# Latent attention on Trainium2: values as the stationary operand, outputs turned back to tokens by a copy and two transposes

## The chip, the cores and the metric

The kernel runs as one program on one core of a Trainium2 chip. The metric is the device time of one execution in microseconds (us); for a kernel the median of its runs is given. The core has five engines with instruction streams of their own, which meet only at semaphores: TensorE (PE, whose weight loads the profile lists apart as PEld), VectorE (DVE), ScalarE (ACT), GpSimd (POOL) and SyncE (SP, which issues most DMAs). Each engine runs its own stream in order.

## The reference

The reference is two networks, one behind the other, on 512 tokens of width 1024. The first is one block of retention and dilated attention with an MLP; the change doesn't touch it. The second has two layers (depth 2) that take the 512 tokens, called latents here, and 256 context tokens. In each layer four mixers of width 256 stand beside one another, and two of them are attention with four heads of 64 channels:

```python
def neighbourhood_attention(q, k, v, k_ctx, v_ctx, rpb, rows):      # "neighbour" unit
    ...
    p = jax.nn.softmax(jnp.concatenate([s_loc, s_ctx], axis=-1), axis=-1).astype(v.dtype)
    ...
    o = jnp.einsum('bhrqik,brikhd->brqhd', p_loc, v_band) + jnp.einsum('bhrql,blhd->brqhd', p_ctx, v_ctx)

def diff_attend(q1, q2, k1, k2, v, lam):                            # "differential" unit
    ...
    p = jax.nn.softmax(s1, axis=-1) - lam * jax.nn.softmax(s2, axis=-1)
    return jnp.einsum('bhqk,bkhd->bqhd', p.astype(v.dtype), v)

def diff_post(o, g, lam_init):
    y = rms_norm_2(o, g) * (1 - lam_init)
    return y.reshape(o.shape[0], o.shape[1], GROUP_W)
```

For 128 latent queries a neighbour unit has 256 local and 256 context keys, a differential unit 512 latent and 256 context keys. The output of the differential unit is then normalised per head (rms over its 64 channels). All of this is float32.

## The kernel before, in words

**Big products.** Nearly all of the time goes to the projections and MLPs. `mm3` (L214 to L218) computes each float32 product as three products of type fp32r, with both operands split into a high and a low part; these are the lines L216, L217 and L218 of the profile. Weights arrive by DMA in `wr`, ACT makes `wh` (L156) and DVE makes `wl` (L145).

**Attention on the latents.** `attention` (L1660) runs once in each layer and so twice in the program. `units` (L1625) walks over four heads, four blocks `qb` of 128 queries, and the two units neighbour and differential: 32 units in a layer, 64 in both. Each unit first makes its scores in PSUM (tiles `s`, lines L1448 to L1459 and L1520, fp32r products), takes the row maximum on DVE (L1452, L1461, L1521) and the exponential on ACT (L142, tiles `f`, `ne`, `wl` in SBUF), with the row sum beside it; a reciprocal on DVE (L1466, L1523) gives one over the sum. The differential unit joins its two maps on DVE (L152, `ne`).

Only two units later (`AHEAD = 2`) does the unit's second half run, `values`. `attend_values` (L1416) transposes the probabilities on PE, block by block of 128 keys (L1424, into PSUM tile `tr`, of which there are two buffers), copies them to SBUF (`wh`, L1426 on DVE or L1428 on ACT), and multiplies (L1430): the transposed probabilities of 128 keys by 128 queries are the stationary operand, and a slice of the values moves, 128 columns wide, which are two heads; half of the result, 64 columns, is then used. The product is float32, has four blocks of keys in a neighbour unit (`hc` or `big`, and `cvn`) and six in a differential unit (`vd`, `cvd`), and stands in the profile as two records for each instruction. Its result `po` has queries on partitions. DVE scales it by the reciprocal into `tok` in the neighbour unit (L1470, listed as L149), ACT in the differential unit (L1531, listed as L142), and ACT squares it (`nj`) for the norm, whose sum it reads out.

**Behind it.** `diff_norm` (L1540) scales the differential outputs, once for heads 0 to 2 and once for head 3. Then `gather` (L1688) transposes `tok` to channels on partitions (L1698) and the output projection begins, with the projected k-tiles that don't depend on attention first.

**Order.** The order in which `units` writes the work is not the order on the engines: the instructions of each engine are put in order when the program is built, by the framework's estimate of when each one could start. It is fixed from then on. The context's own attention (`context`, tiles `npt`, `cst`) uses the same functions earlier in the program, interleaved with projections.

Of the kernel before, what the change touches and what calls it, by code (L numbers as in the profile page):

```python
# [82 lines left out]
class Net:  # L83
# [1332 lines left out]
    def attend_values(self, e, vs, head, po, eng=None):  # L1416

        nk = e.shape[1] // P
        pt = self.t([P, nk, P], self.soft["pt"])
        for b0 in range(0, nk, 4):  # L1420
            n = min(4, nk - b0)
            tp = self.ps((P, n, P), "tr")
            for i in range(n):
                self.nc.tensor.transpose(tp[:, i], e[:, (b0 + i) * P:(b0 + i + 1) * P], self.ident)  # L1424
            if eng and b0 == 0:
                self.nc.vector.tensor_copy(pt[:, b0:b0 + n], tp)  # L1426
            else:
                self.nc.scalar.copy(pt[:, b0:b0 + n], tp)  # L1428
        for kb in range(nk):
            self.nc.tensor.matmul(po, lhsT=pt[:, kb], rhs=vs[kb][:, head // 2 * P:(head // 2 + 1) * P],  # L1430
                                  start=kb == 0, stop=kb == nk - 1)
        return po[:, head % 2 * 64:(head % 2 + 1) * 64]

    def neighbour(self, yn, head, qb, qn, kx, kc, st, vx, vc, bt, po):

        nc = self.nc
        pair, odd = divmod(head, 2)
        rs = slice(odd * 64, (odd + 1) * 64)
        (qh, ql), (kch, kcl) = qn[pair], kc[pair]
# [12 lines left out]
        nc.vector.tensor_reduce(out=sm[:, 0:1], in_=ps[:, nl:], axis=AX.X, op=ALU.min)  # L1452
        vs, low = vc, sm[:, 0:1]
        if nl:
            w0 = WINDOW[qb]
            kh, kl = [k.rearrange("p (r c) -> p r c", c=64)[:, :, w0:w0 + 32] for k in (kh2, kx[pair][1])]
            out = ps[:, :nl].rearrange("p (r c) -> p r c", c=32)
            mm(out, lhsT=qs2[:, qs], rhs=kh, start=True, stop=False)
            mm(out, lhsT=qh[odd][:, qs], rhs=kl, start=False, stop=True)  # L1459
            low = sm[:, 1:2]  # L1460
            nc.vector.tensor_tensor_reduce(  # L1461
                out=ps[:, :nl], in0=ps[:, :nl], in1=bt[:, (qb + 1) // 2].rearrange("p r c -> p (r c)"), scale=1.0,
                scalar=sm[:, 0:1], op0=ALU.add, op1=ALU.min, accum_out=low)
            vs = [vx[:, qb, 0], vx[:, qb, 1]] + vc
        self.act(e, ps, AF.Exp, bias=low, scale=-1.0, accum_out=sm[:, 5:6])
        nc.vector.reciprocal(out=sm[:, 6:7], in_=sm[:, 5:6])  # L1466

        def values():
            o = self.attend_values(e, vs, head, po, qb % 2)
            self.ts(yn[:, qb, head * 64:(head + 1) * 64], o, sm[:, 6:7], ALU.mult)  # L1470
        return values

# [35 lines left out]
    def differential(self, s, yd, ssq, head, qb, qst, kst, vs, c, po):  # L1508
        nc = self.nc
        nk = kst.shape[2]  # L1510
        cuts = [(k0, min(k0 + 512, nk)) for k0 in range(0, nk, 512)]
        qs = slice(qb * P, (qb + 1) * P)
        sm = self.t([P, 16], "dsm")
        em = []
        for mp in range(2):
            b = mp * 8
            e = self.t([P, nk], self.soft["e"][mp])
            ps = self.ps((P, nk), self.soft["s2"])
            for k0, k1 in cuts:
                nc.tensor.matmul(ps[:, k0:k1], lhsT=qst[:, mp, qs], rhs=kst[:, mp, k0:k1], start=True, stop=True)  # L1520
            nc.vector.tensor_reduce(out=sm[:, b + 2:b + 3], in_=ps, axis=AX.X, op=ALU.max, negate=True)  # L1521
            self.act(e, ps, AF.Exp, bias=sm[:, b + 2:b + 3], accum_out=sm[:, b + 3:b + 4])
            nc.vector.reciprocal(out=sm[:, b + 6:b + 7], in_=sm[:, b + 3:b + 4])  # L1523
            em.append(e)

        self.stt(sm[:, 15:16], sm[:, 14:15], c["nlam"], sm[:, 3:4], ALU.mult, ALU.mult)
        self.stt(em[0], em[1], sm[:, 15:16], em[0], ALU.mult, ALU.add)

        def values():
            o = yd[:, qb, head * 64:(head + 1) * 64]  # L1530
            self.act(o, self.attend_values(em[0], vs, head, po), scale=sm[:, 6:7])  # L1531
            junk = self.t([P, 64], "nj")
            self.act(junk, o, AF.Square, accum_out=ssq[:, head, qb:qb + 1])
            if head == 3 and qb == 0 and not s.ctx:
                self.diff_norm(s, yd, ssq, 0, 3)
            if head == 3 and qb == s.nt - 1:
                self.diff_norm(s, yd, ssq, 0 if s.ctx else 3, 4)
        return values

    def diff_norm(self, s, yd, ssq, h0, h1):  # L1540

        n = h1 - h0
        v = self.t([P, n, s.nt], "rs_vd")
        self.ts(v, ssq[:, h0:h1], -0.5 / 64, ALU.mult, -0.5 * EPS, ALU.add)
        r = self.rsqrt(v.rearrange("p h t -> p (h t)"), n * s.nt).rearrange("p (h t) -> p h t", h=n)
        for h in range(h0, h1):
            o = yd[:, :, h * 64:(h + 1) * 64]
            self.tt(o, o, r[:, h - h0].unsqueeze(2).to_broadcast([P, s.nt, 64]), ALU.mult)
# [76 lines left out]
    def units(self, s, c, po, st, more, vx, vc, vd, bts):  # L1625

        todo = []
        for head in range(4):
            if head == 0:
                ssq = self.t([P, 4, s.nt], "ssq")  # L1630
                t = self.t([P, 2, s.nt, 256], "tokc" if s.ctx else "tok")
                s.yn, s.yd = t[:, 0], t[:, 1]
            for qb in range(s.nt):
                i = 2 * (qb % 2)
                for unit in range(2):
                    if unit:
                        todo.append(self.differential(s, s.yd, ssq, head, qb, st[head][0], st[head][1], vd, c, po[:, i + 1]))
                    else:
                        todo.append(self.neighbour(s.yn, head, qb, s.qn, None if s.ctx else s.kv[0], self.ckv[0], st[head],
                                                   vx, vc, bts[head], po[:, i]))  # L1640
                    if len(todo) > AHEAD:
                        todo.pop(0)()
                    if qb == 0 and unit and head < 3:
                        more(head + 1)
                    yield
        for values in todo:
            yield values

    def context(self, s, c):

# [8 lines left out]

    def attention(self, s, l, c, ne):  # L1660
        self.soft = {"e": ("ne", "wl"), "s2": "s2", "s1": "s1", "pt": "wh"}
        self.open("soft", ne=ne, nsm=5, dsm=5, ssq=2, nj=2)
        self.psum(SOFT_PS)
        po = self.ps((P, 4, P), "po")
        ckv = self.ckv
        vc = [ckv[1][:, i] for i in range(2)]
        vd = [s.kv[3][:, i] for i in range(s.nt)] + [ckv[3][:, i] for i in range(2)]
        st, bts = s.st, [self.nbias(l, 0)]

        def more(head):  # L1670
            bts.append(self.nbias(l, head))
            st.append(self.stacks(s, head))
        todo = [v for v in self.units(s, c, po, st, more, s.kv[1], vc, vd, bts) if v]
        self.gather_start(s)
        for values in todo:
            values()
        self.close("soft")
        self.close("heads")
        self.psum(GEMM_PS)
# [249 lines left out]
```

## Time and profile before

| | before |
|---|---|
| median of 3 runs | 2801.17 us (2799.91 to 2804.06) |
| the profiled execution: its time, its span | 2802.46 us, 2800.7 us |
| granted TensorE clock, mean | 0.996 of full speed |
| busy share of the span: PE, PEld, DVE, ACT, POOL | 98%, 84%, 61%, 38%, 2% |
| DMA | 354.74 MB, mean 127 GB/s |

A row of a group view names line, engine, operation and tiles (out<-in), then the shape, the count, the busy time in us, the mean of one in ns, and the idle time of the engine just before, with what ended it. A row of a timeline gives the start in us from the beginning of the span, the time from there to the last end in us, the engine, the line, what it writes and reads, and how many instructions of one kind are merged in it; idle time before it stands in brackets with what ended it. PE's instructions overlap in such a row: the distance from one start to the next is what one costs, and the length of a single record is longer.

### The profile page before, as it was taken

The page shows a single profiled execution, that of the slowest core. Times are in us where ns is not written, and L with a number is a line of the kernel's source. Part 1 is how long each engine was busy: PE and PEld are TensorE (multiplying, and loading weights), DVE is VectorE, ACT ScalarE, POOL GpSimd, SP SyncE. Part 2 cuts the span into 40 slices and gives each one's busy share as a digit, 9 for nine tenths or more (in the row PEclk, how much of TensorE's full clock was granted, in tenths as well). Part 3 has the DMA queues.
Part 4 walks back from the last instruction along what each step waited for, and adds up shares of the span by engine and source line. Part 5 has one row for each costly group of instructions (what it writes and reads, how often), then busy time and mean ns, then how long its engine had stood idle before and what let it go on. Part 6 is the DMA issues. An engine that isn't in the chain of part 4 may idle for free.

```text
span 2800.7 us, 38389 instructions
## 1 busy us (share of the span) xinstructions
PE 2738.2 (98%) x15332; PEld 2354.6 (84%) x15332; DVE 1716.0 (61%) x3205; ACT 1057.5 (38%) x1969; POOL 62.3 (2%) x109
## 2 busy tenths in 40 slices
PE   8999999999999999999998999999999999999998
PEld 4888888988888888789887888888889988888887
DVE  6667777353567888788768564444446858644434
ACT  4433433333334223245647332222224538433323
POOL 3000000000020000000000000000000000000000
PEclk9999999999999999999999999999999999999999
DMA  7355343343354555755443421112122443323231
GB/s 273 127 198 165 136 152 128 120 127 97 116 180 163 181 185 196 236 168 169 136 116 89 128 62 61 61 61 73 63 68 92 133 134 93 126 95 102 91 105 61
DMA packets 275203, 354.74 MB, mean 127 GB/s; under 512 B 19320, under 2 KB 221170, under 8 KB 274768
## 3 DMA queue, kind: packets, MB, share of 16 engines
q1 hardware_dynamic: 259744, 323.58, 36.5%
q0 software_dynamic: 4384, 13.99, 1.6%
q10 hardware_dynamic: 10896, 14.72, 1.6%
q8 instruction: 121, 1.98, 0.3%
q14 instruction: 58, 0.48, 0.1%
HBM read 318.62 MB, written 23.65 MB: 122 GB/s over the span
## 4 chain that ended last, share of the span: by engine, by line
PE 83%; DVE 6%; DMA 4%; ACT 3%; issue 2%; POOL 1%; ACTq 0%; SPq 0%; DVEq 0%; POOLq 0%
PE mm L216 25%; PE mm L217 25%; PE mm L218 25%; DMA wr<-in_ada_w 2%; PE po L1430 2%; DVE ada L152 2%; DVE wl L145 1%; PE at L216 1%; ACT wh L156 1%; PE tr L1424 1%; DMA wr<-in_w_ff 1%; PE tr L398 1%; PE at L217 1%; PE at L218 1%; DVE dsm L1521 1%
## 5 line engine op out<-in xcount | busy, mean ns | idle before, releaser
L156 ACT CAST wh<-wr 128x1024 fp32r<-128x1024 f32 (+1 forms) x442 | 425.7, 970 | 822.3 <-PE mm L217 662.0
L145 DVE TENSOR_TENSOR wl<-wr,wh 128x1024 fp32r<-128x1024 f32 (+1 forms) x442 | 493.7, 1122 | 343.6 <-ACT wh L156 335.5
L216 PE MATMUL mm<-h,wh 128*128 128x512 f32 (+1 forms) x1712 | 652.1, 383 | 3.3 <-ACT h L142 2.4
L217 PE MATMUL mm<-h,wh 128*128 128x512 f32 (+1 forms) x1712 | 652.1, 382 | 0.4 <-DVE h L152 0.4
L218 PE MATMUL mm<-h,wl 128*128 128x512 f32 (+1 forms) x1712 | 650.3, 381 | 0.5 <-DVE wl L145 0.5
L216 PEld LDWEIGHTS mm<-h,wh 128*128 128x128 f32 x1712 | 321.6, 188 | 64.4 <-ACT h L142 3.5
L217 PEld LDWEIGHTS mm<-h,wh 128*128 128x128 f32 x1712 | 322.2, 188 | 62.6 <-DVE ada L152 3.4
L218 PEld LDWEIGHTS mm<-h,wl 128*128 128x128 f32 x1712 | 322.3, 188 | 60.3 <-DVE wl L145 0.9
L217 PE MATMUL mm<-mid,wh 128*128 128x512 f32 (+1 forms) x864 | 330.7, 383 | 0.9 <-DVE mid L145 0.9
L216 PE MATMUL mm<-mid,wh 128*128 128x512 f32 (+1 forms) x864 | 330.4, 383 | 0.0
L218 PE MATMUL mm<-mid,wl 128*128 128x512 f32 (+1 forms) x864 | 329.5, 381 | 0.0
L152 DVE SCALAR_TENSOR_TENSOR ada<-wr,cs,ada 128x1024 f32<-128x1024 f32 x168 | 212.4, 1279 | 37.0 <-DMA wr<-in_ada_w 25.3
L216 PE MATMUL mm<-wh,h 128*128 128x256 f32 x704 | 200.0, 284 | 0.0
L217 PE MATMUL mm<-wl,h 128*128 128x256 f32 x704 | 199.7, 284 | 0.0
L218 PE MATMUL mm<-wh,h 128*128 128x256 f32 x704 | 199.6, 284 | 0.0
L142 ACT ACTIVATE f<-mm 128x256 f32<-128x256 f32 (+2 forms) x192 | 99.5, 520 | 256.9 <-PE mm L218 256.7
L217 PEld LDWEIGHTS mm<-mid,wh 128*128 128x128 f32 x864 | 162.5, 188 | 32.9 <-DVE mid L145 2.2
L218 PEld LDWEIGHTS mm<-mid,wl 128*128 128x128 f32 x864 | 162.5, 188 | 31.1
L216 PEld LDWEIGHTS mm<-mid,wh 128*128 128x128 f32 x864 | 162.5, 188 | 30.6
L145 DVE TENSOR_TENSOR f<-f 128x512 f32<-128x512 f32 (+2 forms) x172 | 99.4, 585 | 143.5 <-ACT f L142 142.3
L152 DVE SCALAR_TENSOR_TENSOR x<-mm,modx,x 128x512 f32<-128x512 f32 (+1 forms) x116 | 84.8, 731 | 166.8 <-PE mm L218 165.4
L217 PEld LDWEIGHTS mm<-wl,h 128*128 128x128 f32 x704 | 134.8, 191 | 0.7 <-issue 0.2
(470 smaller groups left out, 4209.6 us busy)
## 6 DMA issues: line engine op xcount, KB each, us to landing
wr<-in_w_ff SPq DMA_DIRECT2D x96, 1024.0 KB
wr<-in_w_in SPq DMA_DIRECT2D x69, 1024.0 KB
wr<-in_ada_w SPq DMA_DIRECT2D x48, 1024.0 KB
wr<-in_w_ada SPq DMA_DIRECT2D x16, 1024.0 KB
wr<-in_w_in SPq DMA_DIRECT2D x24, 512.0 KB
awr<-in_w_ada SPq DMA_DIRECT2D x16, 512.0 KB
wr<-in_w_ret_out SPq DMA_DIRECT2D x8, 1024.0 KB
wr<-in_w_out SPq DMA_DIRECT2D x8, 1024.0 KB
```

The lines of the kernel that those rows point to most:

```text
L142: return self.nc.scalar.activation(out=out, in_=in_, func=func, **kw)
L145: return self.nc.vector.tensor_tensor(out=out, in0=a, in1=b, op=op)
L152: return self.nc.vector.scalar_tensor_tensor(out=out, in0=a, scalar=s, in1=b, op0=op0, op1=op1)
L156: self.nc.scalar.copy(hi, src)
L216: mm(out, lhsT=ah, rhs=bh, start=start, stop=False)
L217: mm(out, lhsT=ah, rhs=bl, start=False, stop=False)
L218: mm(out, lhsT=al, rhs=bh, start=False, stop=stop)
L398: when(self.nc.tensor.transpose(ps[:, j], acc[:, m * P:(m + 1) * P], self.ident))
L1424: self.nc.tensor.transpose(tp[:, i], e[:, (b0 + i) * P:(b0 + i + 1) * P], self.ident)
L1430: self.nc.tensor.matmul(po, lhsT=pt[:, kb], rhs=vs[kb][:, head // 2 * P:(head // 2 + 1) * P], start=kb == 0, stop=kb == nk - 1)
L1521: nc.vector.tensor_reduce(out=sm[:, b + 2:b + 3], in_=ps, axis=AX.X, op=ALU.max, negate=True)
```

## The change

For the latents (not the context), `attend_values` swaps the operands: 64 columns of the values, those of the one head, become the stationary operand, and the transposed probabilities move. The result has 64 channels on partitions and 128 queries in columns. The neighbour unit writes partitions 0 to 63 of `po`, the differential unit 64 to 127, and `po` holds four query blocks. The two scalings per block are gone. After every second block a new function, `token_major`, copies `po` of both units and two query blocks to SBUF on ACT (128x256), transposes it with two PE transposes into a `tr` buffer, and one DVE product with the reciprocals of both units (kept in a new tile `rden`) writes `tok`; ACT squares the differential half as before. The first part of `token_major`, the copy, follows the values at once; the transposes and what is behind them follow one unit later. `diff_norm` for heads 0 to 2 is called at the end of head 2.

```diff
@@ attend_values
+        turn = po.shape[0] == 64
+        cols = slice(head * 64, head * 64 + 64) if turn else slice(head // 2 * P, (head // 2 + 1) * P)
         for kb in range(nk):
-            self.nc.tensor.matmul(po, lhsT=pt[:, kb], rhs=vs[kb][:, head // 2 * P:(head // 2 + 1) * P],
-                                  start=kb == 0, stop=kb == nk - 1)
-        return po[:, head % 2 * 64:(head % 2 + 1) * 64]
+            a, b = pt[:, kb], vs[kb][:, cols]
+            if turn:
+                a, b = b, a
+            self.nc.tensor.matmul(po, lhsT=a, rhs=b, start=kb == 0, stop=kb == nk - 1)
+        return po if turn else po[:, head % 2 * 64:(head % 2 + 1) * 64]
@@ neighbour
-        nc.vector.reciprocal(out=sm[:, 6:7], in_=sm[:, 5:6])
+        nc.vector.reciprocal(out=self.rden[head % 2][:, qb, 0:1] if nl else sm[:, 6:7], in_=sm[:, 5:6])
         def values():
             o = self.attend_values(e, vs, head, po, qb % 2)
+            if nl:
+                return
             self.ts(yn[:, qb, head * 64:(head + 1) * 64], o, sm[:, 6:7], ALU.mult)
@@ differential
         def values():
+            if not s.ctx:
+                self.attend_values(em[0], vs, head, po)
+                return
...
+    def token_major(self, s, ssq, head, half, po):
+        nc = self.nc
+        ev = self.t([P, 2, P], "f")
+        nc.scalar.copy(ev, po[:, half])
+        yield
+        tp = self.ps((P, 2, P), "tr")
+        for i in range(2):
+            nc.tensor.transpose(tp[:, i], ev[:, i], self.ident)
+        qs = slice(half * 2, half * 2 + 2)
+        out = s.tok[:, :, qs, head * 64:(head + 1) * 64]
+        self.tt(out.rearrange("p u q r -> p q u r"), tp.rearrange("p q (u r) -> p q u r", u=2),
+                self.rden[head % 2][:, qs].unsqueeze(3).to_broadcast([P, 2, 2, 64]), ALU.mult)
+        junk = self.t([P, 2, 64], "nj")
+        o = out[:, 1]
+        for i in range(2):
+            self.act(junk[:, i], o[:, i], AF.Square, accum_out=ssq[:, head, half * 2 + i:half * 2 + i + 1])
+        if head == 2 and half:
+            self.diff_norm(s, s.yd, ssq, 0, 3)
+        if head == 3 and half:
+            self.diff_norm(s, s.yd, ssq, 3, 4)
+        yield
@@ units
+                    if turn:
+                        dst = po[unit * 64:(unit + 1) * 64, qb // 2, qb % 2]
...
+                    if back:
+                        next(back.pop(0))
@@ attention
-        self.open("soft", ne=ne, nsm=5, dsm=5, ssq=2, nj=2)
+        self.open("soft", ne=ne, nsm=5, dsm=5, ssq=2, nj=1, rden0=1, rden1=1)
...
-        po = self.ps((P, 4, P), "po")
+        po = self.ps((P, 2, 2, P), "po")
```

What this does to the order of PE is seen in the middle of the first layer's attention. Before, in one block of queries (PE; `po` is the product with the values, `tr` are transposes, `s` scores):

```order
L1430 MATMUL po<-hc,wh 128x128 x2
L1430 MATMUL po<-cvn,wh 128x128 x2
L1424 MATMUL tr<-ident,ne 128x128 x2
L1520 MATMUL s_13748<-h 128x256
L1448 MATMUL s_13718<-h 128x256
L1449 MATMUL s_13718<-ckn,qn 128x256
L1424 MATMUL tr<-ident,f 128x128 x3
L1430 MATMUL po<-vd,wh 128x128 x4
L1430 MATMUL po<-cvd,wh 128x128 x2
L1458 MATMUL s_13718<-h 128x256
```

Now, in the same block (L1435 is the product with the values, written 64x128; L1452 to L1463 and L1526 are the score lines, L1558 is the new transpose):

```order
L1435 MATMUL po<-wh,hc 64x128 x2
L1435 MATMUL po<-wh,cvn 64x128 x2
L1424 MATMUL tr<-ident,ne 128x128 x2
L1435 MATMUL po<-wh,vd 64x128 x4
L1526 MATMUL s_13752<-h 128x512
L1452 MATMUL s_13716<-h 128x256
L1453 MATMUL s_13716<-ckn,qn 128x256
L1435 MATMUL po<-wh,cvd 64x128 x2
L1526 MATMUL s_13752<-h 128x256
L1558 MATMUL tr<-ident,f 128x128 x2
```

The products with the values are now 64 columns wide and stand in three runs in this block, each with work of the full 128 columns before and behind it; before there were two runs, as wide as all else around them.

The second place is the end of the first layer's attention on DVE (`wl` is the weight split for the output projection, `rs_vd` begins the last `diff_norm`). Before:

```order
L149 TENSOR_SCALAR tok<-po,nsm 128x64 [waits PE_49,Activation_49]
L145 TENSOR_TENSOR hc<-yc,hc 128x256 x2
L145 TENSOR_TENSOR wl<-wr,wh 128x1024 [waits DMAHW6_49,Activation_49]
L145 TENSOR_TENSOR wl<-wr,wh 128x1024 [waits Activation_49]
L145 TENSOR_TENSOR wl<-wr,wh 128x1024 [waits DMAHW7_49,Activation_49]
L149 TENSOR_SCALAR rs_vd<-ssq 128x4 [waits Activation_49]
```

Now:

```order
L145 TENSOR_TENSOR wl<-wr,wh 128x1024 [waits DMAHW6_49,Activation_49]
L145 TENSOR_TENSOR wl<-wr,wh 128x1024 [waits Activation_49]
L145 TENSOR_TENSOR tok<-tr,rden_13285 128x2x2x64 [waits PE_49]
L145 TENSOR_TENSOR wl<-wr,wh 128x1024 [waits DMAHW7_49,Activation_49]
L149 TENSOR_SCALAR rs_vd<-ssq 128x4 [waits Activation_49]
```

The last writing of `tok` has moved from ACT (and, for the neighbour unit, from ahead of the weight splits) to DVE behind two weight splits, and the squares that feed `rs_vd` wait for it.

## Rows read from the trace of the kernel before

**Rows 1.** The page's busy times and shares of the span.

```profile
PE 2738.2 (98%) x15332; PEld 2354.6 (84%) x15332; DVE 1716.0 (61%) x3205; ACT 1057.5 (38%) x1969; POOL 62.3 (2%) x109
```

**Rows 2.** Windows over both attention stages: length, busy us per engine (instructions), clock, DMA.

```profile
1454.70:1542.60 87.90, 79.06 (x592) 69.17 (x592) 75.85 (x200) 70.51 (x188) 0.00 (x0) 1.00 0.36 94
2296.40:2387.80 91.40, 81.75 (x601) 71.86 (x600) 78.19 (x203) 72.30 (x190) 0.00 (x0) 0.98 0.38 96
```

**Rows 3.** Longest wait of PE in the first stage: us in total, times, longest.

```profile
PE po L1430 <- ACT wh L1428: 3.4, 6, 1.4
```

**Rows 4.** Timeline, PE: float32 products and transposes back to back.

```profile
1485.39 1.06 PE L1430 MATMUL po<-vd,wh 128*128 128x128 f32 x8
...
1492.07 0.60 PE L1424 MATMUL tr<-ident,ne 128*128 128x128 f32 x4
...
2226.35 1.03 PE L1305 MATMUL at<-tok,wst 128*128 128x256 f32 x4
```

**Rows 5.** Timeline, PE: products of 64 rows among products of 128.

```profile
1295.08 0.40 PE L216 MATMUL mm<-wh,hc 128*128 128x256 f32 x2
1295.41 0.38 PE L216 MATMUL at<-ckn,cqn 64*128 64x256 f32 x1
1295.63 0.28 PE L217 MATMUL at<-ckn,cqn 64*128 64x256 f32 x1
1295.95 0.38 PE L217 MATMUL mm<-wl,hc 128*128 128x256 f32 x1
1296.17 0.28 PE L218 MATMUL mm<-wh,hc 128*128 128x256 f32 x1
```

**Rows 6.** Timeline, PE: float32 products with one stationary column among others.

```profile
41.34 1.88 PE L375 MATMUL at<-awr,cs 128*1 128x512 f32 x4
43.15 0.50 PE L217 MATMUL mm<-h,wh 128*128 128x512 f32 x1
43.48 0.39 PE L218 MATMUL mm<-h,wl 128*128 128x512 f32 x1
43.72 0.39 PE L216 MATMUL mm<-h,wh 128*128 128x512 f32 x1
...
44.64 0.40 PE L218 MATMUL mm<-h,wl 128*128 128x512 f32 x1
44.97 1.88 PE L375 MATMUL at<-awr,cs 128*1 128x512 f32 x4
46.78 0.66 PE L398 MATMUL tr<-ident,ada 128*128 128x128 f32 x4
```

**Rows 7.** Groups of weight loads over the program: one stationary column, and 128.

```profile
L375 PEld LDWEIGHTS at<-awr,cs 128*1 128x1 f32 x32 | 2.1, 84 | 13.5 <-issue 8.2 <-DMA awr<-in_w_ada 4.8 <-DMA sp_x<-x 0.4
L1430 PEld LDWEIGHTS po<-vd,wh 128*128 128x128 f32 x256 | 31.5, 191 | 7.5 <-ACT wh L1428 3.5 <-issue 2.2 <-ACT wh L156 1.2
```

**Rows 8.** Groups of ACT and DVE in the first attention stage.

```profile
L1428 ACT COPY wh<-tr 128x256 f32<-128x256 f32 x16 | 6.0, 374 | 2.3 <-PE tr L1424 2.2
L142 ACT ACTIVATE tok<-po,dsm 128x64 f32<-128x64 f32 x16 | 5.0, 315 | 6.1 <-PE po L1430 6.1
L149 DVE TENSOR_SCALAR tok<-po,nsm 128x64 f32<-128x64 f32 x16 | 4.4, 276 | 1.6 <-PE po L1430 1.5
L145 DVE TENSOR_TENSOR tok<-tok,rs_y 128x256 f32<-128x256 f32 x3 | 1.1, 415 | 0.0
```

**Rows 9.** Timeline of all engines at the first stage's end, cut.

```profile
1537.97 0.63 PE L1424 MATMUL tr<-ident,ne 128*128 128x128 f32 x4 [1.61 <-DVE ne L152]
...
1540.39 1.13 PE L1430 MATMUL po<-vd,wh 128*128 128x128 f32 x8 [0.47 <-DVE tok L149]
1540.83 3.49 DVE L145 TENSOR_TENSOR wl<-wr,wh 128x1024 fp32r<-128x1024 f32 x3
...
1542.60 1.09 PE L1698 MATMUL at<-ident,tok 128*128 128x128 f32 x8 [0.63 <-ACT tok L142]
...
1544.27 0.66 PE L1698 MATMUL at<-ident,tok 128*128 128x128 f32 x4
```

More of the change, by code (lines that the diff above doesn't have):

```diff
@@ L1522, in differential @@
             self.act(e, ps, AF.Exp, bias=sm[:, b + 2:b + 3], accum_out=sm[:, b + 3:b + 4])
-            nc.vector.reciprocal(out=sm[:, b + 6:b + 7], in_=sm[:, b + 3:b + 4])
+            out = sm[:, b + 6:b + 7]
+            if mp == 0 and not s.ctx:
+                out = self.rden[head % 2][:, qb, 1:2]
+            nc.vector.reciprocal(out=out, in_=sm[:, b + 3:b + 4])
             em.append(e)
@@ L1533, in values @@
             self.act(junk, o, AF.Square, accum_out=ssq[:, head, qb:qb + 1])
-            if head == 3 and qb == 0 and not s.ctx:
-                self.diff_norm(s, yd, ssq, 0, 3)
             if head == 3 and qb == s.nt - 1:
-                self.diff_norm(s, yd, ssq, 0 if s.ctx else 3, 4)
+                self.diff_norm(s, yd, ssq, 0, 4)
         return values
+    def token_major(self, s, ssq, head, half, po):
[19 more added lines that the diff above has]
+        yield
     def diff_norm(self, s, yd, ssq, h0, h1):
@@ L1627, in units @@
         todo = []
+        turn = not s.ctx
+        if turn:
+            self.rden = [self.t([P, 4, 2], "rden%d" % i) for i in range(2)]
+        back = []
         for head in range(4):
@@ L1631, in units, with both @@
                 t = self.t([P, 2, s.nt, 256], "tokc" if s.ctx else "tok")
-                s.yn, s.yd = t[:, 0], t[:, 1]
+                s.tok, s.yn, s.yd = t, t[:, 0], t[:, 1]
             for qb in range(s.nt):
-                i = 2 * (qb % 2)
                 for unit in range(2):
+                    if turn:
+                        dst = po[unit * 64:(unit + 1) * 64, qb // 2, qb % 2]
+                    else:
+                        dst = po[:, 2 * (qb % 2) + unit]
                     if unit:
-                        todo.append(self.differential(s, s.yd, ssq, head, qb, st[head][0], st[head][1], vd, c, po[:, i + 1]))
+                        vals = self.differential(s, s.yd, ssq, head, qb, st[head][0], st[head][1], vd, c, dst)
+                        if turn and qb % 2:
+                            def both(vals=vals, head=head, half=qb // 2):
+                                vals()
+                                back.append(self.token_major(s, ssq, head, half, po))
+                                next(back[-1])
+                            todo.append(both)
+                        else:
+                            todo.append(vals)
                     else:
                         todo.append(self.neighbour(s.yn, head, qb, s.qn, None if s.ctx else s.kv[0], self.ckv[0], st[head],
-                                                   vx, vc, bts[head], po[:, i]))
+                                                   vx, vc, bts[head], dst))
+                    if back:
+                        next(back.pop(0))
                     if len(todo) > AHEAD:
@@ L1646, in units @@
         for values in todo:
-            yield values
+            yield lambda values=values: (back and next(back.pop(0)), values())
+        if turn:
+            yield lambda: [next(part) for part in back]
     def context(self, s, c):
```

## Prediction

> **What bounds the kernel now.** The page comes first: PE is busy for 98% of the span [rows 1], so whatever lengthens or shortens PE's work shows in the time unless a wait of PE takes it up. The change lies in two stages only, the latent attention of either layer, so the windows over these come next, each from the first long scores to the gathering transposes [rows 2]: 87.90 us with PE busy for 79.06, and 91.40 us with 81.75. PE stands idle there for 8.84 + 9.65 = 18.5 us; ACT (70.5 and 72.3) and DVE (75.9 and 78.2) are close behind it, and the granted clock is 1.00 and 0.98, the level of 2.4 GHz. Then the waits: PE waits most for ACT's copy of the transposed probabilities, 3.4 us in six waits [rows 3], the lag of a pipeline of three busy engines. Last the stage's end, where nothing is left to fill in: waits of 1.61, 0.47 and 0.63 us [rows 9], 2.7 together, which I double to 5.4 for both stages. So 18.5 - 5.4 = 13.1 us of PE's idle time can take up more work, and all beyond that must lengthen the kernel.
>
> **The stream of the values costs what it did.** Eight float32 records of 128 moving columns take 1.06 us with a last record of some 0.28, so one comes every 0.11 us; with 256 columns four take 1.03, of which 0.38 is the last, so 0.22 each [rows 4]. The pace goes with the moving columns. Before, 128 columns of values moved; now 128 queries move. The product count stays at ten in each pair of units, so 64 units keep 640 records at 0.11 us. A weight load of one column takes 84 ns and of 128 columns 191 [rows 7], so one of 64 is some 138; it lies under the stream already, and I take no gain (at most 0.003 us a record, 1.9 us, if the load is what holds the pace a little above the 0.108 that half of 256 columns gives).
>
> **What the narrow products cost: switches of the array's shape.** A result of 64 partitions puts the array into another shape than the 128 columns of the scores and transposes around it. The trace shows such switches in dense work. Three products of 64 rows: the start before them is at 1295.20, the first comes 0.21 us later instead of 0.12, the second after 0.22; they leave with 0.32 for two starts instead of 0.24, and then 0.22 [rows 5]. The same with a narrow stationary operand, one column: it begins 0.33 us after the product before it, where the pace is 0.24 (43.48 to 43.72), and its own starts are then at the pace of its 512 columns, 0.43 (1.88 less 0.59, over three); the next product comes 0.52 after the last of them instead of 0.43, and the one behind after 0.33 instead of 0.23; where transposes follow, they are late by 0.09, and their first three starts take 0.39 instead of 0.33 [rows 6]. I read: each switch holds the stream by 0.09 us, and the first load behind it is not hidden, which costs 0.10 for 128 columns of a product, 0.06 for a transpose and nothing for one column. For 64 columns, between nothing and 0.10, I take the middle, 0.05, since the loads lie in the middle too (138 ns between 84 and 191 [rows 7]). The Trainium skill, "TensorEngine Tiling (Array Packing)", Tiling Modes, Key Properties, says that changing the tiling mode drains TensorE; the trace agrees, with the 0.09 us, and nothing above rests on the sentence.
>
> In PE's order of the changed kernel the narrow products stand in 94 runs over both stages (three runs in most blocks, as in the piece shown): 64 are followed by transposes, 30 by scores. One run costs 0.09 + 0.05 on entry and 0.09 + 0.06 or 0.09 + 0.10 on leaving: 64 x 0.29 + 30 x 0.33 = 28.5 us. Bounds: with the 64-column load at 0 it is 23.8, at 0.10 it is 33.2.
>
> **The new transposes.** Sixteen pieces of two: 32 x 0.11 [rows 4] = 3.5 us of PE.
>
> **ACT and DVE.** ACT loses 32 scalings of 315 ns, 10.1 us, and gains 16 copies of 128x256 at 374, 6.0 us [rows 8]: 4.1 us less. DVE loses 32 scalings of 276 ns, 8.8, and gains 16 products of 128x256; the same size costs 415 ns [rows 8], 6.6 us: 2.2 less. Both sit beside PE, which waits for them less; as PE is the bound this is worth nothing of its own and goes into what PE's idle time can take up. The reciprocals only write elsewhere, the squares keep their number and size.
>
> **The end of each stage.** PE's next wait is at the first transposes of `tok`: before, they start at 1542.60, when ACT's scaling has ended [rows 9]; now the copy (374 against 315 ns) releases the two new transposes there, so this start stays within 0.1 us. But the last product into `tok` is on DVE behind two weight splits of 3.49 / 3 = 1.16 us, begun at 1540.83, so it ends near 1543.6 at best; ACT squares twice behind it, and only then copies the first gathered tile, for which PE waits before its second set of transposes. That set began at 1544.27 [rows 9]; by this chain (1543.6, some 0.9 for two squares, some 0.6 for the copy) it begins near 1545.3, while the transposes in between make PE later by 0.2 only. I take 1.3 us in each stage, 2.6 together, between 0 (PE is late by as much anyway) and twice that.
>
> **The sum.** 28.5 + 3.5 + 2.6 = 34.6 us more on PE. Of the 13.1 us of idle time that can go I let 11 go: with some 16 us more on PE in a stage, ACT and DVE have that much more room, and a drain in front of a product that waits anyway is free. 34.6 - 11 = 23.6. The profiled execution took 2802.5 us, 1.8 more than its span, which makes 2826.1; it lies 1.3 above the median of 2801.2, on which I forecast 2824.8, so **2825 us**.
>
> **Rivals.**
> 1. *Engines beside PE give back more.* PE's idle time goes altogether (13.1), the 64-column load is hidden (23.8 for the switches) and the end costs nothing, while ACT's 4.1 us shorten waits at the end too: 23.8 + 3.5 - 13.1 - 4.1 = 10, 2811 us. For it: ACT and DVE are nearly as busy as PE [rows 2]. Against: PE then has no idle time at all inside a stage.
> 2. *Not slower: the switches are free in float32 work of this width, and the evacuations decide.* Then PE gains 3.5 + 2.6 of work, which its idle time takes up, and ACT's 4.1 us come off the waits: 2797 us. It decides as soon as a run costs less than (13.1 - 6.1) / 94 = 0.07 us. Against: every switch in the trace, by rows and by columns, costs more on either side [rows 5, 6].
> 3. *Both halves of the array at once.* Neighbour products use columns 0 to 63 and differential ones 64 to 127. If four of ten ran beside the other six, 32 x 4 x 0.22 = 28 us would go, 2825 - 28 = 2797 or, with fewer switches, some 2780. The Trainium skill has this in the same section: different tiles can execute in parallel. Against: in PE's order no neighbour product stands next to a differential one; transposes or scores of full width are always between.
> 4. *More than the sum.* Nothing is taken up, the load costs 0.10 and the ends 5.2: 33.2 + 3.5 + 5.2 = 42, 2843 us. For it: the order is fixed at the build by estimates, and with other true durations it fits worse; the new transposes also share the two `tr` buffers.
> 5. *The change doesn't do what it says.* The order shows 32 new transposes, 16 copies and 16 products, and no scaling of `po` by 64 columns in the latent stages, so this has no chance of its own.
>
> **How the numbers follow.** The forecast has 0.70, rival 1 0.12, rival 2 0.05, rival 3 0.02, rival 4 0.11. The forecast's own range, from the bounds of the load (4.7 either way) and of the taken-up idle time (0 to 13.1), is 2815 to 2836. The whole range reaches down to a little under rival 1 and half way to rival 4: 2808 to 2839. A measurement of this kernel tells 0.2%, 5.6 us, from no change. Slower: forecast, rival 4 and most of rival 1, 0.90. Within 0.2%: most of rival 2 and a little of rival 1, 0.06. Faster: rival 3 and a rest of rival 2, 0.04.
>
> **What the profile after would show.** Right: records of L1435 still 0.11 us apart within a run, the first some 0.09 late and the second some 0.05; transposes and scores behind a run late by 0.09 and then 0.06 to 0.10; both windows longer by 10 to 13 us with PE's idle time in them shrunk; ACT's and DVE's busy time down by about 4 and 2; all other stages alike. The forecast is wrong if a run's neighbours keep their pace (rival 2), if records of the two halves overlap (rival 3), or if the windows grow by more than 17 us each with new waits of PE for `tr` or `tok` (rival 4).

## The result, and the profile after

The changed kernel takes **2835.7 us** (median of 4 runs, 2832.7 to 2840.8) against 2800.5 for the kernel before (2799.4 to 2804.1): the ratio is 1.0128, 95% interval 1.0116 to 1.0140. That is 35 us slower; 24 were forecast. The time lies inside the whole range (2808 to 2839), at the upper end of the forecast's own (2815 to 2836). The profiled execution took 2836.0 us with a span of 2834.2, which is 33.5 us more than before.

The page's busy line, which answers to [rows 1]:

```profile
PE 2763.1 (97%) x15364; PEld 2354.9 (83%) x15364; DVE 1712.8 (60%) x3189; ACT 1054.3 (37%) x1953; POOL 62.1 (2%) x109
```

ACT and DVE have each lost 3 us (4.1 and 2.2 were forecast), and PE has gained 25. Where: the windows of [rows 2] began some microseconds behind the first long scores in the first stage and 1 us behind them in the second, so here both kernels are cut anew, each from its first long scores to its first gathering transposes. First the kernel before (length, then busy us of PE, PEld, DVE, ACT, POOL with instruction counts, granted clock, DMA share, GB/s):

```profile
1450.20:1542.60 92.40, 81.98 (x606) 71.31 (x607) 79.54 (x208) 73.19 (x194) 0.00 (x0) 1.00 0.38 96
2295.20:2387.80 92.60, 82.94 (x606) 72.77 (x606) 78.97 (x204) 72.30 (x190) 0.00 (x0) 0.98 0.38 96
```

The changed kernel, the same view:

```profile
1448.70:1558.20 109.50, 95.12 (x623) 71.95 (x624) 78.26 (x199) 70.80 (x183) 0.00 (x0) 0.98 0.32 81
2311.80:2421.50 109.70, 96.67 (x622) 73.12 (x623) 77.70 (x196) 70.42 (x180) 0.00 (x0) 0.97 0.32 81
```

Each stage is 17.1 us longer, 34.2 together; all that lies outside adds up to -0.7. PE's idle time in the stages (length less busy) has not shrunk but grown, from 10.4 + 9.7 to 14.4 + 13.0 us.

The switches of the array's shape are seen in PE's timeline of the changed kernel (start, length, then the group):

```profile
1461.93 0.38 PE L1435 MATMUL po<-wh,cvn 128*64 128x128 f32 x2
1462.24 0.44 PE L1424 MATMUL tr<-ident,ne 128*128 128x128 f32 x2
1462.61 0.43 PE L1435 MATMUL po<-wh,vd 128*64 128x128 f32 x2
...
1464.41 0.65 PE L1435 MATMUL po<-wh,cvd 128*64 128x128 f32 x4
1464.99 0.39 PE L1462 MATMUL s<-cqn 128*128 128x256 f32 x1
1465.22 0.28 PE L1463 MATMUL s<-hc,qn 128*128 128x256 f32 x1
```

Two transposes between two runs of narrow products hold the stream for 0.37 us (1462.24 to 1462.61) where two starts of 0.11 make 0.22: 0.06 for the first load and 0.09 for the next switch. The run of four behind it takes 0.58 us to the next score, and the second score comes 0.23 later. The same place in the kernel before:

```profile
1465.17 0.61 PE L1430 MATMUL po<-cvd,wh 128*128 128x128 f32 x4
1465.54 0.36 PE L1458 MATMUL s<-cqn 128*128 128x256 f32 x1
1465.74 0.28 PE L1459 MATMUL s<-hc,qn 128*128 128x256 f32 x1
```

There it is 0.37 and 0.20. The difference of 0.24 is the forecast's 0.05 for the first load and 0.19 for leaving to a score. Priced so on the starts of PE in both stages, the 94 runs cost 28.6 us; 28.5 were forecast. That is a gross sum. The starts that are late, by less than 0.13 us against the pace of their sort and of whatever cause, add up to 8.9 us in the stages of the kernel before and to 28.4 in those of the changed one, 19.5 more: some 30 of the runs begin behind a wait, where the switch can't be told from it, and first loads that were not hidden cost the products of the kernel before some 3.7 us too (4.7 now).

The waits of PE in the first stage (us in total, times, longest), which answer to [rows 3], and then those of the second stage that are new:

```profile
PE po L1435 <- ACT wh L1428: 3.6, 8, 0.8
...
PE s L1452 <- ACT f L142: 2.2, 2, 1.3
PE tr L1424 <- DVE tok L145: 1.5, 2, 1.0
...
PE tr L1558 <- ACT f L1554: 0.9, 2, 0.5
...
PE tr L1424 <- DVE tok L145: 1.1, 2, 1.0
PE tr L1558 <- ACT f L1554: 0.9, 2, 0.5
```

Transposes of probabilities now wait for the division that reads a `tr` buffer (L145), and the transposes back wait for the copy that feeds them (L1554): 2.4 us in the first stage, 2.0 in the second. No such wait stood in the kernel before. As large is the growth of an old one: the neighbour unit's scores wait 2.2 and 1.8 us for exponentials that still read their bank, where the kernel before had this once, for 0.4 us.

The granted clock differs a little too. Windows of the changed kernel around a stretch at the lower level:

```profile
1502.30:1505.70 3.40, 1.72 (x9) 1.15 (x10) 3.36 (x11) 1.94 (x6) 0.00 (x0) 1.00 0.71 165
1505.70:1509.10 3.40, 3.40 (x15) 3.08 (x16) 2.05 (x8) 2.05 (x8) 0.00 (x0) 0.50 0.22 51
```

PE had been busy for only 1.72 of 3.4 us, with one of those waits for exponentials, 1.28 us long; then the clock stood at 0.50, the level of 1.2 GHz, and rose again. One such stretch lay in the stages of before (mean clock 1.00 and 0.98), three lie there now (0.98 and 0.97). Measured on the starts of records in them, they cost 3.5 us more than before.

So the 34.2 us: switches 28.6 (gross), 32 transposes back 3.5, the two new waits 4.4, the clock 3.5, less 5.8. The last figure is what is left over, and it holds several things: a slightly faster stream (some 2 us), the first loads that the kernel before paid too (3.7), and against them the grown waits. Behind the windows come the stages' ends. The first, which answers to [rows 9]:

```profile
1558.19 1.04 PE L1750 MATMUL at<-ident,tok 128*128 128x128 f32 x8
...
1560.78 0.65 PE L1750 MATMUL at<-ident,tok 128*128 128x128 f32 x4 [1.31 <-ACT f L142]
```

The second set of gathering transposes begins 2.59 us behind the first set; before it was 1.67. PE now waits 1.31 us for it, and did not wait there before. The second layer, first in the kernel before and then in the changed one:

```profile
2387.84 1.09 PE L1698 MATMUL at<-ident,tok 128*128 128x128 f32 x8 [0.78 <-ACT tok L142]
...
2389.70 0.60 PE L1698 MATMUL at<-ident,tok 128*128 128x128 f32 x4
```

```profile
2421.51 1.04 PE L1750 MATMUL at<-ident,tok 128*128 128x128 f32 x8
2422.30 0.48 PE L216 MATMUL mm<-h,wh 128*128 128x512 f32 x1
2423.62 0.66 PE L1750 MATMUL at<-ident,tok 128*128 128x128 f32 x4 [0.84 <-ACT f L142]
```

The second set comes 2.11 us behind the first instead of 1.86, but only one product of the output projection stands between the sets, where four stood before, and PE waits 0.84 us. At equal work (16 of these transposes and 40 products) PE is 0.8 us later than before; in the first layer, after 12 transposes and 30 products, it is 1.4.

### The profile page after: what moved, and what is told of

The parts are those of the page before. It is cut to its first block, busy times and chain, and to the rows that moved or that the text cites. A ratio compares the mean times of both kernels' runs of the same rounds, so it can differ in the third digit from the quotient of the medians.

```text
span 2834.2 us, 38404 instructions
## 1 busy us (share of the span) xinstructions
PE 2763.1 (97%) x15364; PEld 2354.9 (83%) x15364; DVE 1712.8 (60%) x3189; ACT 1054.3 (37%) x1953; POOL 62.1 (2%) x109
## 5 line engine op out<-in xcount | busy, mean ns | idle before, releaser
L145 DVE TENSOR_TENSOR wl<-wr,wh 128x1024 fp32r<-128x1024 f32 (+1 forms) x442 | 493.6, 1121 | 347.4 <-ACT wh L156 335.6
L145 DVE TENSOR_TENSOR f<-f 128x512 f32<-128x512 f32 (+2 forms) x172 | 99.3, 585 | 141.7 <-ACT f L142 140.5
```

Source lines behind the costliest of these rows:

```text
L145: return self.nc.vector.tensor_tensor(out=out, in0=a, in1=b, op=op)
```

## The experiments

Theory A: the added time is the switches of the array's shape, at full price. Theory B: it is the new copies, transposes and the buffers they hold. The kernel before, timed beside each of them, had medians of 2798 to 2799 us. The ratio's interval for the changed kernel is 1.0116 to 1.0140, so times that differ from it by 3 to 5 us are not clear of noise.

### No narrow products

```diff
-        turn = po.shape[0] == 64
-        cols = slice(head * 64, head * 64 + 64) if turn else slice(head // 2 * P, (head // 2 + 1) * P)
+        turn = nk == 6 or self.turn
+        cols = slice(head // 2 * P, (head // 2 + 1) * P)
...
-                        dst = po[unit * 64:(unit + 1) * 64, qb // 2, qb % 2]
+                        dst = po[:, unit, qb % 2]
...
-        nc.scalar.copy(ev, po[:, half])
+        for u in range(2):
+            nc.scalar.copy(ev[u * 64:u * 64 + 64], po[head % 2 * 64:head % 2 * 64 + 64, u])
```

> Everything of the change is kept (values stationary, copies, transposes back, one division) but the stationary operand is the whole pair of heads, 128 columns, so that the product fills the whole array and no product of 64 columns is left; half of its rows are thrown away and the copy is made in two pieces of 64 partitions (8 more ACT copies of about 0.32 us in each stage, beside PE). Theory A (the 94 changes of the array's shape at about 0.30 us each are the loss): 2835.7 - 28.5 = 2807 us, range 2802 to 2812. Theory B (the loss is in the copies, the transposes back and the buffers that they hold): 2833 to 2842, since all of these stay and ACT gets more. Theory C (both share it): 2816 to 2826.

Measured: 2810.1 us, ratio 1.0038 (1.0024 to 1.0051). The stages of this kernel:

```profile
1445.20:1542.40 97.20, 84.50 (x623) 72.98 (x624) 79.49 (x200) 73.53 (x192) 0.00 (x0) 1.00 0.36 92
2296.30:2392.50 96.20, 85.01 (x622) 72.91 (x623) 79.20 (x196) 72.47 (x188) 0.00 (x0) 1.00 0.36 93
```

Of the two stages 12.3 and 13.5 us are gone, and 25.6 us of the loss of 35 are back, inside the range of theory A. Not all of it is the switches. Late starts of under 0.13 us fell by 17.8 us, to 10.6; the clock is 1.00 throughout, where the changed kernel had 10.2 us at half (up to 5 us of work); and PE's idle time is 3.5 us less. Whether the clock and the waits came back because the switches went is not shown, so theory A has at least half of the loss directly, and up to some three quarters. The stages remain 4.8 and 3.6 us longer than before: 1.7 each for the transposes, and most of the rest is PE's idle time, 2.3 and 1.5 us more (PE waits 6.5 us in the first stage for the copied probabilities). That much of theory B is real, and the copies are dearer here, being 16 and not 8 in a stage.

### Fewer, longer runs

```diff
-        for kb in range(nk):
+        kbs = list(range(4, nk)) + list(range(4)) if turn else list(range(nk))
+        for kb in kbs:
```

> The changed kernel with one edit: the differential's six products of a unit start with the two blocks that are copied last, so that its products wait for both copies and then stand together more often: 64 runs of 64-column products instead of 94. Theory A: 30 runs fewer at 0.30 us = 9 us less, 2827 us (2823 to 2831), less what the later start costs. Theory B: no gain from fewer runs, and all products now wait for the second copy: 2835 to 2845.

Measured: 2832.2 us, ratio 1.0115 (1.0101 to 1.0129), 3.5 less than the changed kernel, between the ranges of the two theories. The switches fell by 9.3 us, priced as above for 30 runs, but PE's waits of over 0.13 us rose by 4.5: a row of this kernel's first stage shows the sort that the changed kernel did not have there.

```profile
PE tr L1424 <- ACT wh L1428: 2.1, 6, 0.6
```

A run that starts later holds up the transposes behind it, and they the copies; that is a reading of the order. The price of a run does not show in this time.

### Ten products together

The products of both units of a query block are issued together, once all is copied; in a second form they alternate between the units: the list is then (4, 0, 5, 1, 6, 2, 7, 3, 8, 9), and each product starts and stops at its first and last block.

```diff
+    def products(self, head, a, b):
+        cols = slice(head * 64, head * 64 + 64)
+        todo = [(u, kb, len(u[1])) for u in (a, b) for kb in range(len(u[1]))]
+        todo = [todo[i] for i in (8, 9, 0, 1, 2, 3, 4, 5, 6, 7)]
+        for (pt, vs, po), kb, nk in todo:
+            self.nc.tensor.matmul(po, lhsT=vs[kb][:, cols], rhs=pt[:, kb], start=kb == (4 if nk == 6 else 0), stop=kb == 3)
...
-                self.attend_values(em[0], vs, head, po)
+                self.products(head, self.half, self.attend_values(em[0], vs, head, po))
```

> The changed kernel with the products of a query block's neighbour and differential attention issued together, ten of them, after both units' transposes and copies: 35 runs of 64-column products instead of 94, same products. The two units' products stand one after the other. Theory A: 59 runs fewer at 0.30 us = 18 us less, 2818 us (2812 to 2823) if the waits stay. Theory B: 2833 to 2845.

> As the kernel with ten products together (here 36 runs), but the products of the two units alternate, so that successive products stand on the two halves of the array's columns. If the halves cannot work at once (the trace of the changed kernel shows 0.109 us a record in a run, but there successive products stood on one half): as that kernel within 3 us, about 2818. If they can: four of each five products pair up, up to 0.22 us for each of 128 pairs in a stage pair of layers = 256 pairs x 0.22 x half = some 28 us less, about 2790. If a change of the half within a run costs a switch of its own (9 more in each run at 0.1 to 0.3 us, some 300 in all): 2848 to 2900.

Measured: 2814.9 us (1.0052; 1.0039 to 1.0065) and 2816.3 us (1.0060; 1.0047 to 1.0072). The first agrees with theory A in time, the second with halves that cannot work at once. The timelines show otherwise. In the second form:

```profile
1463.92 0.27 PE L1446 MATMUL po<-wh,vd 128*64 128x128 f32 x1
1463.93 0.27 PE L1446 MATMUL po<-wh,hc 128*64 128x128 f32 x1
1464.03 0.27 PE L1446 MATMUL po<-wh,vd 128*64 128x128 f32 x1
1464.04 0.27 PE L1446 MATMUL po<-wh,cvn 128*64 128x128 f32 x1
...
1468.74 0.32 PE L1446 MATMUL po<-wh,vd 128*64 128x128 f32 x1 [0.28 <-ACT wh L1428]
...
1470.20 0.66 PE L1424 MATMUL tr<-ident,f 128*128 128x128 f32 x4
```

Records of the differential unit (columns 64 to 127) and of the neighbour unit (columns 0 to 63) start 0.01 us apart, and a pair comes every 0.11 us: **both halves of the array work at once**. The whole run of ten, from its first start to the transposes behind it, takes 1.46 us. This is the mechanism of the forecast's third rival. The Trainium skill states it in "TensorEngine Tiling (Array Packing)", Tiling Modes, Key Properties (tiles operate independently), and here the trace agrees. The form that doesn't alternate does it as well:

```profile
1464.44 0.32 PE L1446 MATMUL po<-wh,cvd 128*64 128x128 f32 x1 [0.22 <-ACT wh L1428]
1464.45 0.32 PE L1446 MATMUL po<-wh,hc 128*64 128x128 f32 x1
```

There two products with `cvd` stand ahead of the first with `hc` in PE's order, and yet its first record starts beside theirs. So "each engine runs its own stream in order", as said at the beginning, does not hold for PE across the two halves. Some 13 us of stream go in a stage in both kernels, beside 9 us of switches; but PE's waits, counted between starts, grew from 18.7 us in a stage to 25 to 28, and the time at the lower clock in both stages from 10 us to 14 and 27, so that the stages still take 97 to 100 us. My expectation of 2790 for working halves was wrong by that, and that the first form came out near theory A's 2818 is chance: the theory knew neither the overlap nor these losses.

### The transposes back in another bank

```diff
-        tp = self.ps((P, 2, P), "tr")
+        tp = po[:, half]
```

> The changed kernel with one edit: the transposes back to tokens write into the bank of the values that the copy has just read, not into one of the two buffers that the transposes of the probabilities use. In the changed kernel such transposes waited 1.5 and 1.1 us in the two stages for the division that holds that buffer (the product of tr and rden). The scheduler moves other instructions with it: 81 runs of 64-column products instead of 94. Theory A with waits that are caused by that buffer: 13 x 0.30 + 2.6 = 6.5 us less, 2829 us (2826 to 2832), and the wait of transposes for the division is gone from the trace. Rival (the wait is the latency of a chain in order, and turns up under another name): only the runs count, 3.9 less or nothing, 2831 to 2837.

Measured: 2830.6 us, ratio 1.0110 (1.0096 to 1.0124), 5.1 less than the changed kernel. The wait of `tr` for the division is gone, but the first stage has it under another name, as large:

```profile
PE po L1435 <- DVE tok L145: 1.5, 2, 0.8
```

There 22.5 us of waits stand instead of 18.7, in the second stage 16.9 instead of 18.7. The switches fell by 3.5 us. The time lies in the first range and 0.4 us below the rival's. The waits, 2 us more in all, speak for the rival: this buffer is not what sets them.

### Half the moving columns in the kernel before

```diff
-            self.nc.tensor.matmul(po, lhsT=pt[:, kb], rhs=vs[kb][:, head // 2 * P:(head // 2 + 1) * P],
+            self.nc.tensor.matmul(po[:, :64], lhsT=pt[:, kb], rhs=vs[kb][:, head * 64:(head + 1) * 64],
```

> The kernel before with one edit: its moving values are the 64 columns of the head itself instead of the 128 columns of the pair, of which half is thrown away. The stationary operand stays 128 wide and the array's shape never changes. If a record of these products is set by the weight load of 128 columns (about 0.11 us a record in the trace of before), the time stays: 2797 to 2802. If the moving columns set it, half of 0.11 us goes from each of 1280 records less what the load still shows: up to 50 us less, 2750 to 2790.

Measured: 2833.5 us, ratio 1.0120 (1.0106 to 1.0134): neither. The pace of the products is as the first reading says, but the kernel is 34 us slower. Timeline, first at the full clock and then further on:

```profile
1464.24 1.00 PE L1430 MATMUL po<-vd,wh 128*128 128x64 f32 x8
1465.08 0.61 PE L1430 MATMUL po<-cvd,wh 128*128 128x64 f32 x4
...
1537.47 1.80 PE L1430 MATMUL po<-vd,wh 128*128 128x64 f32 x8
1539.06 1.06 PE L1430 MATMUL po<-cvd,wh 128*128 128x64 f32 x4
```

Eight records take 0.84 us and then, of the same sort, 1.59. (The expectation counts 1280 records; the two stages have 640, so its largest gain should have read half of that.) The windows tell why (both stages, then one stretch):

```profile
1449.70:1558.90 109.20, 92.56 (x606) 82.42 (x606) 80.19 (x207) 71.82 (x192) 0.00 (x0) 0.87 0.32 82
2314.10:2417.20 103.10, 86.85 (x607) 74.79 (x607) 79.10 (x204) 71.92 (x189) 0.00 (x0) 0.94 0.34 86
...
1531.40:1538.20 6.80, 6.32 (x28) 6.01 (x29) 4.46 (x15) 3.62 (x9) 0.00 (x0) 0.50 0.00 0
```

A mean of 0.87 over 109.2 us between levels of 1.00 and 0.50 is 28 us at 1.2 GHz, and 0.94 over 103.1 is 12: up to 20 us of work lost, against 2 in the kernel before. PE's idle time rose by 6.2 and 6.6 us as well. The build's scheduler also placed instructions a little otherwise; how much of the loss comes from that, and why the clock stayed low for so long, was not separated.

### Later, and on one half

Both have exactly 32 runs of ten, one unit later (what is appended below is issued behind the next neighbour unit's transposes), in a fixed order; the second, with the last line of the diff, puts both units on the same half.

```diff
-                self.products(head, self.half, self.attend_values(em[0], vs, head, po))
+                self.pend.append([head, self.half, self.attend_values(em[0], vs, head, po), None])
...
-                        dst = po[unit * 64:(unit + 1) * 64, qb // 2, qb % 2]
+                        dst = po[0:64, unit, qb % 2]
```

> As the kernel whose ten products of a query block alternate between the array's halves, with two differences: they are issued one unit later, behind the next neighbour unit's transposes, so that the copies have time, and the order of transposes, products and the neighbour's second scores is held as written: exactly 32 runs of ten. The trace of that kernel showed pairs of records that start 7 ns apart and 0.11 us from pair to pair (some 13 us less in a stage), and waits of 28 us in a stage instead of 18.7. Theory D (both halves work at once; the gain was eaten by waits for copies, which the later issue hides): waits fall to about 18 us in a stage, 2816 - 20 = 2796 us, range 2788 to 2803. Rival (the stage is set by latencies and the copies, whatever PE saves): 2808 to 2818.

> As the kernel with the products one unit later, in 32 runs of ten, but both units' products stand on the same half of the array (and the copy is made in two pieces). Same products, same number of changes of shape. Theory D: nothing can run at once, so the 13 us of each stage come back: 26 us above the kernel with the products one unit later, near 2822 if that is at 2796, and no records 7 ns apart. Rival (the short distances in the trace are only how records are written, and the gain of putting ten together came from fewer runs alone): within 4 us of it.

Measured: 2822.9 us (1.0083; 1.0069 to 1.0097) and 2825.3 us (1.0095; 1.0079 to 1.0110). Theory D falls on the time: 2.4 us lie between them, not 26, and the first lies above both ranges that were given for it. It holds on the records: none of the second kernel's start 0.01 us apart, and its stream is 25 us longer in the two stages. Nor are the short distances only how records are written, for the work behind a run begins later too, 2.33 us after the run's first start instead of 1.46:

```profile
1481.90 0.65 PE L1455 MATMUL po<-wh,hc 128*64 128x128 f32 x4
...
1484.23 0.39 PE L1471 MATMUL s<-h 128*128 128x256 f32 x1
```

First the stages of the kernel with both halves, then of that with one (its profiled execution took 2820.2 us, 5 less than its median):

```profile
1449.10:1551.00 101.90, 79.69 (x622) 61.95 (x623) 78.78 (x198) 69.44 (x183) 0.00 (x0) 0.93 0.34 87
2305.20:2407.80 102.60, 82.39 (x622) 64.69 (x623) 77.45 (x195) 69.37 (x179) 0.00 (x0) 0.90 0.34 87
```

```profile
1450.30:1551.30 101.00, 88.41 (x623) 73.31 (x624) 79.00 (x199) 73.08 (x191) 0.00 (x0) 0.97 0.35 88
2304.80:2405.50 100.70, 88.02 (x623) 72.47 (x624) 78.12 (x195) 71.25 (x187) 0.00 (x0) 0.98 0.35 88
```

PE is busy for 14 us less with both halves, and the stages are no shorter: it is idle for 17 us more, and the clock of 0.93 and 0.90 (34 us at the lower level against 10) takes up to 12 us of work. The wait that grew most in the first stage, from the first kernel and then the second:

```profile
PE s L1547 <- ACT ne L142: 11.1, 7, 2.7
```

```profile
PE s L1547 <- ACT ne L142: 3.2, 3, 1.5
```

Scores wait for the exponentials that empty their banks. My reading is that, with PE's products made cheap, the chain of scores, maximum, exponential and mix beside PE sets these stages in this order. Shown is that neither ACT nor DVE is full (69 and 78 of some 102 us), and that PE waits for them.

### Three units ahead

```diff
-AHEAD = 2
+AHEAD = 3
```

> The kernel with ten products together (35 runs, 2814.9 us, waits of 27.1 and 25.1 us in the two stages against 15.6 in the kernel before) with one edit: the values start one unit later (three units stand between scores and values instead of two); 37 runs. If the waits are latencies that distance hides, they fall towards 16 us where buffers allow (the second layer has four buffers for the differential's probabilities, the first two): 5 to 10 us less there, 2805 to 2810, which would still not pass the kernel before; if both layers gain, 2795 to 2800. Rival (the stages are set by the chain through ACT and DVE, as the kernels with and without overlapped halves suggest, which took 101 to 103 us a stage alike): 2812 to 2820, or slower where buffers are short.

Measured, on the first form of the ten together: 2820.7 us, ratio 1.0080 (1.0067 to 1.0094), 0.7 us above the rival's range. Its stages:

```profile
1442.80:1549.10 106.30, 86.30 (x622) 68.19 (x623) 79.77 (x199) 71.61 (x184) 0.00 (x0) 0.87 0.33 84
2303.50:2402.10 98.60, 81.08 (x622) 60.69 (x623) 78.60 (x196) 70.69 (x180) 0.00 (x0) 0.97 0.35 90
```

The second layer, with four buffers, takes 98.6 us (97.1 with two units ahead), and PE is idle there for 17.5 us (16.2): the distance hides nothing. The first, with two buffers, takes 106.3 (97.8), but its clock was 0.87 instead of 0.98, up to 12 us of work, and PE's idle time grew by only 1.4 us; so the clock can account for all of it, and the buffers' part is not shown. No version tried passes the kernel before.

## Why the prediction was right, and where it was not

**The switches: right in mechanism and price, gross.** Entry 0.09 + 0.05 and exit 0.09 + 0.06 or 0.09 + 0.10, taken from three products of 64 rows and a few of one column [rows 5, 6], hold for 64 columns, and their sum is within 0.1 us of what the starts give at the same prices. The load, estimated at 138 ns, is one row of the first stage:

```profile
L1435 PEld LDWEIGHTS po<-wh,vd 128*64 128x64 f32 x128 | 13.5, 136 | 5.2 <-ACT wh L1428 3.7 <-issue 1.3 <-ACT f L142 0.2
```

What the sum left out is that the kernel before paid for late starts as well, so that the net is nearer 20 us than 28. The kernel without narrow products gets 25.6 us back, of which 17.8 are late starts; the rest is clock and waits.

**The stream: right.** The pace went from 0.112 to 0.109 us a record, the small gain that was bounded at 1.9 us. The sentence that the pace goes with the moving columns holds for 256 against 128 [rows 4], not below: with 64 moving under a full stationary operand it stays at 0.11. That the load sets it there is likely, and not shown.

**The transposes: right**, 3.5 us. **The ends: right**, 2.6 forecast and 2.2 found: the chain by division, squares and copy came as described, and PE is late at equal work by 1.4 us in the first layer and by 0.8 in the second, which I had taken to be alike.

**The step that failed** is "Of the 13.1 us of idle time that can go I let 11 go". None of it went: PE's idle time in the two stages grew by 7.3 us. I had reasoned that ACT and DVE, with 16 us more of time, would be late less often. But the waits are lags in a fixed order, a transpose that waits for a copy, which waits for the last transposes: a slower PE delays both sides of such a wait alike. That is my reading of it; shown is that such waits stay, in the changed kernel (3.6 and 2.9 us for the copied probabilities against 3.4 and 2.0) and without narrow products too. To these the change added waits of its own for the division and the copy (4.4 us), the neighbour scores' waits for exponentials grew by 3.6, and the clock, which the sum held constant, took 3.5. Without the 11 us the sum is 34.6, and the span grew by 33.5. That they lie so close is luck: the switches came out cheaper net than the sum had them, and the new waits and the clock made it up.

**The signs.** The records within and around a run came as described, and ACT's and DVE's busy time fell. But the windows were to grow by 10 to 13 us with PE's idle time shrunk; they grew by 17.1 each, and it grew. By the sign that the prediction set itself, more than 17 us each with new waits for `tr`, this is rival 4's case, if by 0.1 us.

**The rivals.** The first and second counted on idle time too and fell with it. The fourth, nothing taken up, was right in its first clause and in the wait on a `tr` buffer, but not in its dear load or ends; the time lies between it and the forecast, 7 us from the one and 11 from the other. The third was set aside for the right reason, that no neighbour product stands beside a differential one. The mechanism itself exists, and put beside each other they do overlap, but its price was wrong: the 25 us of stream that went did not become time, for PE waited more and its clock fell.

## What to carry to other kernels

Price each change of the array's shape at its two ends, some 0.3 us gross for a run among float32 work of full width here, and count the runs in the final order. Count what the old order pays of the same kind, too. Don't take added work out of the idle time of a bounding engine without a reason for each wait: here none of 13 us went. Narrow products of different halves overlap when they stand next to each other; here that saved 25 us of PE's stream and no time, so look first at what else would have to become faster.

## What the runs showed of the hardware

- Records on different column halves start 0.01 us apart, and a product on one half can start ahead of one that is earlier in PE's order on the other. Ten products take 1.46 us on two halves and 2.33 on one.
- Among float32 work of full width, the start behind a change of the array's shape is 0.09 us late, and the one behind it 0.05 (64-column load) or 0.06 (transpose).
- Halving the moving columns from 128 to 64 under a 128-column float32 stationary operand gave no pace (0.11 us a record).
- The granted clock stood at 0.50 for 3 us in the two stages of the kernel before, for 10 in the changed one, 27 and 34 in the two whose products alternate between the halves, 35 with three units ahead, 40 with half the moving columns, and not at all in the kernel without narrow products. The kernels in which PE was idle for 33 us and more in these stages had 14 to 40 us of it, those with up to 31 had 0 to 14. In the stretch shown PE had been busy for 1.72 of 3.4 us before it fell.
